# Issuing the second half's V gathers at twice the rate per step of their lane

## The chip, the cores and the metric

The kernel runs on one core of a Trainium2 chip. The metric is device time in microseconds (us), the median of several runs of one execution each; lower is better. Engines are named as in the profile: PE is TensorE (matmuls), PEld its weight loads, DVE is VectorE, ACT is ScalarE, POOL is GpSimd, SP is SyncE. DMAs are issued from the queues of SP, ACT and POOL; in this kernel SP issues the weights and most stores, POOL issues gathers and re-layouts.

## What is computed

One encoder block on 512 tokens (8 rows of 64) of width 1024, in float32. Cut to what matters here:

```python
x = x + 0.5 * swiglu(rmsnorm(x, norm_ffn1), w_ffn1_gu, w_ffn1_down)
h = rmsnorm(x, norm_mix)
xr, gr, q, k, v, ga, gb = split(h @ w_in, 7)
y_lru = (rglru_forward(conv(xr)) + rglru_backward(conv(xr))) * gelu(gr)
q, k = per-head rmsnorm of q and k
# for every query row, and for each of 4 blocks of 16 columns: scores against
# 8 rows x 32 columns of keys, a learned bias, a mask, softmax, then p @ v
y_att = neighbourhood_attention(q, k, v, rel_pos_bias)
x = x + (sigmoid(ga) * y_lru + sigmoid(gb) * y_att) @ w_out
x = x + 0.5 * swiglu(rmsnorm(x, norm_ffn2), w_ffn2_gu, w_ffn2_down)
```

There are 16 heads of 64 columns.

## The kernel before, in words

Every matmul is made of three float32r matmuls on a high and a low part (`mm3`, lines 171 to 174), so PE has most of the work. The middle of the kernel computes the projections of `w_in` one after the other and weaves two other pieces of work between their matmuls: the recurrence (`lru`) and the attention (`heads`). The parts of the middle that this change concerns run in this order:

1. Attention is done in two halves of 8 heads each (`hf` 0 and 1, the loop at the end of the attention code). For each half `qk_raw` computes q and k, `v_get` computes v, and `heads` is appended to a list of generators, the lane "att".
2. After both halves, `gates` computes 24 chunks of 24 matmuls of 128x512 (lines 172 to 174) for the gelu gate and the two merge gates, in phase "g". Between and in the middle of those chunks, `weave(RATE["g"])` advances the lanes. So the scores of the attention (line 950), its transposes (918, 920) and its products with V (1013) of the second half all stand between gate matmuls on PE.

A lane is a list of generators. Each call of `weave` adds the lane's rate to the lane's account, and for every whole unit in the account the generator is advanced by one step, that is to its next `yield`:

```python
    def weave(rate):
        for ln, n in rate.items():
            q = lanes[ln]
            due[ln] += n
            while due[ln] >= 1 and q:
                ...
                    next(q[0])
                    due[ln] -= 1
```

The lane "v" holds `v_more(hf)`. It gathers from DRAM the layouts of V that the attention's products need, since `v_get` leaves V there first (`vd`, line 860). It has seven steps. Steps 1 to 3 issue one gather each of 256 KB (`vs`, line 869). Then, for each of the two edge blocks of columns (n = 0, then n = 3), a buffer `te` is cleared by POOL (line 876) and two steps follow, each of which issues three gathers of 64 KB (`va` twice and `ve` once, line 880). All are issued from POOL's queue. For the first half all seven steps are taken at once (`until("v", lambda: False)`); for the second half they come by the rate of phase "g".

For one tile of heads `fi` (two heads, four such tiles in a half) the attention goes: `start` transposes q and k on PE; `scores` computes the scores on PE, DVE adds the bias `bm` (line 970), ACT takes the exponential (977), DVE scales (982); `ship` transposes 32x32 blocks on DVE (991, 992), stores the result to DRAM from SP's queue (`pd`, line 994) and reads it back from POOL's queue in four DMAs of 112 KB for each of the two blocks of columns (`PT`, line 998); `apply` multiplies it with V on PE (line 1013). One `apply` takes its columns in the order n = 0, 1, 2, 3: first `va` and `ve` of the left edge, then `vs`, then `va` and `ve` of the right edge. `bias` fetches the next tile's `bm` from POOL's queue (line 892). In the second half the `apply` of a tile stands two tiles of scores later (`ATT_LAG`).

What sets the order: PE, DVE, ACT, POOL and SP each run their instructions in one fixed order, which a scheduler makes from the order in which the code was written and from priorities. A POOL DMA that has to wait (for its source, for its buffer, or for room in the queue) holds up all that stand behind it on POOL. Buffers of the size of a tile come from one pool of 43 (`big_t`); there are five `PT` buffers and four `bm` buffers.

Of the kernel before, what the change touches and what calls it, by code (L numbers as in the profile page):

```python
# [83 lines left out]
    "xr": {"att": 0.0, "lru": 2.75},  # L84
    "t0": {"att": 0.0, "lru": 3.25},
    "t1": {"att": 0.75, "tail": 0.75, "lru": 2},
    "g": {"att": 0.7, "tail": 0.7, "lru": 1.5, "v": 0.25},
}


# [1123 lines left out]
```

## Time and profile before

| | us |
|---|---|
| median of 3 runs (lowest to highest) | 1114.73 (1114.38 to 1115.2) |
| the profiled execution, its own time | 1114.18 |
| its span, from first to last instruction | 1112.4 |
| DVE busy | 813.2 (73%) |
| ACT busy | 578.0 (52%) |
| POOL busy | 149.3 (13%) |

The mean granted TensorE clock over the span is 0.997. All instants below are microseconds from the start of the span. The gate matmuls of phase "g" run on PE from 550.7 to about 722. A row of the timeline gives the start, the duration, the engine, the line, the operation, its output and inputs, and, in brackets, how long the engine was idle before it and what ended the wait; "issue" means that the engine waited for nothing that the profile shows. A row of the windows view gives for one stretch the busy time of each engine, then the granted clock, the busy share of the DMA engines and the rate.

### The profile page before, as it was taken

What the parts mean: (1) busy time and instruction counts of PE and PEld (TensorE: products, weight loads), DVE (VectorE), ACT (ScalarE), POOL (GpSimd) and SP (SyncE); (2) the same over time, 40 slices, a digit from 0 to 9 for tenths busy, and PEclk for the clock granted to TensorE, in tenths of its full rate; (3) what the DMA queues carried; (4) which work ended last, traced back from release to release, by engine and by line L of the source; (5) the groups of instructions that cost most, each with busy time, mean ns of one, the idle gap of its engine ahead of it and who ended that gap; (6) DMA issues with size and microseconds to landing.
All of it is one profiled execution on the core that took longest, in us unless ns stands there. A gap on an engine that the chain in (4) does not pass through costs nothing.

```text
span 1112.4 us, 17673 instructions
## 1 busy us (share of the span) xinstructions
PE 1100.6 (99%) x6811; PEld 974.8 (88%) x6811; DVE 813.2 (73%) x1295; ACT 578.0 (52%) x871; POOL 149.3 (13%) x243
## 2 busy tenths in 40 slices
PE   9999999999999999999999979999999999999998
PEld 8899999988888778788888868889999999998887
DVE  7878777794745776999877956759877777785542
ACT  8554544563533679877454432346554454564330
POOL 0000000000000351230333542001000000000000
PEclk9999999999999999999999989999999999999999
DMA  8566666643423685573687655377766666553421
GB/s 267 153 169 152 150 156 167 159 147 95 133 82 107 168 255 152 167 210 106 211 260 184 195 176 160 104 239 160 199 146 158 157 166 147 157 170 95 133 76 38
DMA packets 64548, 175.93 MB, mean 158 GB/s; under 512 B 14544, under 2 KB 18384, under 8 KB 64464
## 3 DMA queue, kind: packets, MB, share of 16 engines
q1 hardware_dynamic: 43136, 127.75, 35.5%
q0 software_dynamic: 20752, 46.80, 21.0%
q8 instruction: 53, 0.87, 0.3%
q10 hardware_dynamic: 576, 0.26, 0.1%
q14 instruction: 31, 0.25, 0.1%
HBM read 150.53 MB, written 15.73 MB: 149 GB/s over the span
## 4 chain that ended last, share of the span: by engine, by line
PE 95%; issue 1%; DMA 1%; DVE 1%; POOL 1%; ACT 0%; ACTq 0%; POOLq 0%
PE acc L312 31%; PE acc L172 10%; PE acc L173 10%; PE acc L174 10%; PE aux L312 5%; PE acc L831 4%; PE acc L832 4%; PE acc L833 4%; PE aux L174 4%; PE aux L172 4%; PE aux L173 4%; PE aux L742 1%; PE aux L1013 1%; PE aux L950 1%; PE acc L464 1%
## 5 line engine op out<-in xcount | busy, mean ns | idle before, releaser
L145 ACT ACTIVATE wh<-wraw 128x1024 fp32r<-128x1024 f32 (+3 forms) x224 | 220.3, 988 | 304.2 <-issue 95.0
L148 DVE TENSOR_TENSOR wl<-wraw,wh 128x1024 fp32r<-128x1024 f32 (+3 forms) x236 | 267.0, 1136 | 100.1 <-ACT wh L145 98.8
L312 PE MATMUL acc<-s,wh 128*128 128x256 f32 x1280 | 232.2, 283 | 0.0
L312 PEld LDWEIGHTS acc<-s,wh 128*128 128x128 f32 x1280 | 199.7, 192 | 0.0
L312 PE MATMUL acc<-s,wl 128*128 128x256 f32 x640 | 181.1, 283 | 0.0
L312 PEld LDWEIGHTS acc<-s,wl 128*128 128x128 f32 x640 | 122.9, 192 | 0.0
L172 PE MATMUL acc<-xh,wh 128*128 128x512 f32 x272 | 107.5, 395 | 0.0
L174 PE MATMUL acc<-xh,wl 128*128 128x512 f32 x272 | 106.2, 391 | 0.0
L173 PE MATMUL acc<-xl,wh 128*128 128x512 f32 x272 | 106.1, 390 | 0.0
L312 PE MATMUL acc<-xl,wh 128*128 128x256 f32 x320 | 90.6, 283 | 0.0
L312 PE MATMUL acc<-xh,wl 128*128 128x256 f32 x320 | 90.6, 283 | 0.0
L312 PE MATMUL acc<-xh,wh 128*128 128x256 f32 x320 | 90.5, 283 | 0.0
L831 PE MATMUL acc<-wh,xh 128*128 128x512 f32 x192 | 75.7, 394 | 0.0
L832 PE MATMUL acc<-wh,xl 128*128 128x512 f32 x192 | 74.8, 389 | 0.0
L833 PE MATMUL acc<-wl,xh 128*128 128x512 f32 x192 | 74.8, 389 | 0.0
L148 DVE TENSOR_TENSOR hl<-h,hh 128x512 fp32r<-128x512 f32 x88 | 57.2, 687 | 21.7 <-PE aux L173 21.5
L172 PE MATMUL aux<-hh,wh 128*128 128x512 f32 (+1 forms) x181 | 69.9, 386 | 0.0
L173 PE MATMUL aux<-hl,wh 128*128 128x512 f32 (+1 forms) x181 | 69.9, 386 | 0.0
L174 PE MATMUL aux<-hh,wl 128*128 128x512 f32 (+1 forms) x181 | 69.9, 386 | 0.0
L174 PE MATMUL acc<-hh,wl 128*128 128x512 f32 (+1 forms) x176 | 67.9, 386 | 0.0
L173 PE MATMUL acc<-hl,wh 128*128 128x512 f32 (+1 forms) x176 | 67.9, 386 | 0.0
L172 PE MATMUL acc<-hh,wh 128*128 128x512 f32 (+1 forms) x176 | 67.9, 386 | 0.0
(221 smaller groups left out, 2297.6 us busy)
## 6 DMA issues: line engine op xcount, KB each, us to landing
wraw<-wqkv SPq DMA_DIRECT2D x24, 512.0 KB, 4.5
wraw<-wg SPq DMA_DIRECT2D x24, 512.0 KB, 7.4
wraw<-w1d SPq DMA_DIRECT2D x22, 512.0 KB, 3.7
wraw<-w2s SPq DMA_DIRECT2D x22, 512.0 KB
pair<-w2s SPq DMA_DIRECT2D x22, 512.0 KB, 4.4
wraw<-w2d SPq DMA_DIRECT2D x22, 512.0 KB, 3.6
wraw<-w1s SPq DMA_DIRECT2D x18, 512.0 KB, 3.5
pair<-w1s SPq DMA_DIRECT2D x18, 512.0 KB, 4.7
```

The source lines that it names most:

```text
L145: nc.scalar.activation(H, raw, AF.Copy)
L148: return nc.vector.tensor_tensor(L, raw, H.bitcast(F32), ALU.subtract)
L172: nc.tensor.matmul(ps, wh, xh, start=first, stop=False, skip_group_check=skip)
L173: nc.tensor.matmul(ps, wh, xl, start=False, stop=False, skip_group_check=skip)
L174: mark["mm"] = nc.tensor.matmul(ps, wl, xh, start=False, stop=last, skip_group_check=skip)
L312: mm = nc.tensor.matmul(o, w_[:, c], x_, start=first and m + k == 0 and w_ is H and x_ is xh_, stop=m + k == 4 and w_ is L, skip_group_che ...
L464: nc.tensor.matmul(pre[i], w[i][1][:, s], xh[k], start=k == 0, stop=False)
L742: prev, mm = mm, nc.tensor.matmul(ps[d][b], W[w][o, c], X[x][o], start=x == 1, stop=w + x == 0)
L831: nc.tensor.matmul(pss[j], xh[kk][:, tj], H[:, s], start=kk == 0, stop=False)
L832: nc.tensor.matmul(pss[j], xl[kk][:, tj], H[:, s], start=False, stop=False)
L833: mark["mm"] = nc.tensor.matmul(pss[j], xh[kk][:, tj], L[:, s], start=False, stop=kk == KT - 1)
L950: mm = hold(nc.tensor.matmul(ps[hp][:, cs], q_[o, n * P : (n + 1) * P], keys(k_[o]), start=k_ is kl, stop=q_ is ql))
```

## The change

One number in the table of rates: in phase "g" the lane of the V gathers gets 0.5 per call of `weave` instead of 0.25, so that a step is due at every second call, where it was due at every fourth. A gate chunk makes two calls, one in its middle and one behind it.

```diff
 RATE = {
     "xr": {"att": 0.0, "lru": 2.75},
     "t0": {"att": 0.0, "lru": 3.25},
     "t1": {"att": 0.75, "tail": 0.75, "lru": 2},
-    "g": {"att": 0.7, "tail": 0.7, "lru": 1.5, "v": 0.25},
+    "g": {"att": 0.7, "tail": 0.7, "lru": 1.5, "v": 0.5},
 }
```

On PE, ACT and SP the instructions stand in the same order as before, and on DVE two neighbours change places (a block transpose of line 991 and a split of line 148). On POOL the order changes from the third tile of heads of the first half to the second tile of the second. The rows below are POOL's, in the order of the program; `x4` stands for four DMAs in a row, and the numbers are those of buffers, which differ between the two programs. The first place is around the last `PT` of the first half (`PT_6013` before, `PT_6017` now). Before:

```order
L998 DMA PT_5901<-pd_5899 128x1x224 x4
L892 DMA bm_6325<-rpb 128x640
L869 DMA vs_6018<-vd_82 128x1x512
L892 DMA bm_6327<-rpb 128x640
L869 DMA vs_6111<-vd_82 128x1x512
L998 DMA PT_6013<-pd_6011 128x1x224 x4
L892 DMA bm_6540<-rpb 128x640
L892 DMA bm_6542<-rpb 128x640
L876 MEMSET ve_6330 128x512
L880 DMA va_6329<-vd_82 64x4x64 x2
```

And at the same place now:

```order
L892 DMA bm_6343<-rpb 128x640
L876 MEMSET ve_6023 128x512
L880 DMA va_6022<-vd_82 64x4x64 x2
L880 DMA ve_6023<-vd_82 64x4x64
L880 DMA va_6022<-vd_82 64x4x64 x2
L880 DMA ve_6023<-vd_82 64x4x64
L892 DMA bm_6345<-rpb 128x640
L876 MEMSET ve_6123 128x512
L880 DMA va_6122<-vd_82 64x4x64 x2
L880 DMA ve_6123<-vd_82 64x4x64
L880 DMA va_6122<-vd_82 64x4x64 x2
L998 DMA PT_6017<-pd_6015 128x1x224 x4
```

Eleven of the twelve edge gathers and both clears, which stood behind the first half's last `PT`, now stand ahead of it. The two `vs` that stood just ahead of it have moved further up, ahead of `PT_5684` and `PT_5903`.

The second place is around the `PT` of the second half's first two tiles of heads (`PT_6292` and `PT_6302`, then `PT_6507`, before; `PT_6310` and `PT_6320`, then `PT_6516`, now). Before:

```order
L998 DMA PT_6292<-pd_6290 128x1x224 x4
L998 DMA PT_6302<-pd_6300 128x1x224 x4
L892 DMA bm_6770<-rpb 128x640
L892 DMA bm_6772<-rpb 128x640
L876 MEMSET ve_6609 128x512
L880 DMA va_6608<-vd_82 64x4x64 x2
L880 DMA ve_6609<-vd_82 64x4x64
L880 DMA va_6608<-vd_82 64x4x64 x2
L880 DMA ve_6609<-vd_82 64x4x64
L998 DMA PT_6507<-pd_6505 128x1x224 x4
L998 DMA PT_6517<-pd_6515 128x1x224 x4
```

And now:

```order
L880 DMA ve_6123<-vd_82 64x4x64
L892 DMA bm_6549<-rpb 128x640
L892 DMA bm_6551<-rpb 128x640
L998 DMA PT_6310<-pd_6308 128x1x224 x4
L998 DMA PT_6320<-pd_6318 128x1x224 x4
L892 DMA bm_6770<-rpb 128x640
L892 DMA bm_6772<-rpb 128x640
L998 DMA PT_6516<-pd_6514 128x1x224 x4
L998 DMA PT_6526<-pd_6524 128x1x224 x4
```

The right edge's clear and its six gathers have left the place between `PT_6302` and `PT_6507`; the two `bm` that stood ahead of the left edge's gathers (`bm_6540`, `bm_6542`) now stand just ahead of the second half's first `PT`.

## The prediction, written before the changed kernel ran

> **What bounds the kernel now.** I read the page first, then who PE waits for, then PE's own rows around that wait.
>
> ```profile
> PE 1100.6 (99%) x6811; PEld 974.8 (88%) x6811; DVE 813.2 (73%) x1295; ACT 578.0 (52%) x871; POOL 149.3 (13%) x243
> PE 95%; issue 1%; DMA 1%; DVE 1%; POOL 1%; ACT 0%; ACTq 0%; POOLq 0%
> PE aux L1013 <- DMA va<-vd: 6.9, 2, 4.7
> PE aux L138 <- DVE pol L667: 1.1, 1, 1.1
> ```
>
> PE is busy 99% of the span, and the chain that ended last is 95% PE. So the time changes only where PE's waits or its clock change. The view of waits (total, times, longest) has two for PE in the whole kernel: 1.1 us at the start, and 6.9 us in two pieces in the attention's product (line 1013), for a `va` gather. This is the only place where a change of DMA order alone can gain anything. PE's timeline there:
>
> ```profile
> 639.38 0.44 PE L1013 MATMUL aux<-PT,va 128*64 128x128 f32 x4
> 639.65 0.39 PE L1013 MATMUL aux<-PT,ve 128*64 128x128 f32 x4
> 639.87 1.04 PE L1013 MATMUL aux<-PT,vs 128*64 128x128 f32 x16
> 645.64 0.66 PE L1013 MATMUL aux<-PT,va 128*64 128x128 f32 x2 [4.72 <-DMA va<-vd]
> 648.49 0.44 PE L1013 MATMUL aux<-PT,va 128*64 128x128 f32 x1 [2.20 <-DMA va<-vd]
> ...
> 651.99 0.40 PE L173 MATMUL acc<-xl,wh 128*128 128x512 f32 x1
> ```
>
> It is the second half's first `apply`. Left edge and middle go through at once; at the right edge PE stands 4.72 and then 2.20 us until the gathers of that edge land. POOL's timeline says why they are late:
>
> ```profile
> 606.21 0.66 POOL L998 DMA_DIRECT2D PT<-pd  x1 [3.37 <-issue]
> ...
> 613.65 1.61 POOL L880 DMA_DIRECT2D va<-vd  x2
> ...
> 624.48 2.02 POOL L998 DMA_DIRECT2D PT<-pd  x3 [5.09 <-DMA pd<-pt]
> ...
> 633.09 1.44 POOL L998 DMA_DIRECT2D PT<-pd  x2 [2.38 <-issue]
> 634.52 1.47 POOL L892 DMA_DIRECT2D bm<-rpb  x2
> ...
> 636.44 0.81 POOL L880 DMA_DIRECT2D va<-vd  x1
> ...
> 646.57 0.77 POOL L880 DMA_DIRECT2D ve<-vd  x1
> 647.80 0.69 POOL L998 DMA_DIRECT2D PT<-pd  x1 [0.46 <-issue]
> ```
>
> The left edge's six were issued from 613.65, in time. The right edge's six stand behind eight `PT` and two `bm` and were issued from 636.44 to 646.57, when PE needed them at 640.7.
>
> **The wait's price.** The wait costs more than 6.92, since PE also runs slower behind it:
>
> ```profile
> 640.00:644.00 4.00, 0.92 (x18) 0.67 (x14) 3.62 (x20) 2.10 (x10) 1.05 (x2) 1.00 0.82 282
> 644.00:652.00 8.00, 4.09 (x18) 2.98 (x19) 0.31 (x2) 1.87 (x6) 4.34 (x6) 0.57 0.30 71
> 652.00:656.00 4.00, 4.00 (x19) 3.32 (x18) 2.87 (x5) 1.87 (x3) 1.96 (x3) 1.00 0.53 152
> ```
>
> The granted clock (third number from the end) is 0.57 from 644 to 652 and 1.00 on both sides. So I price the passage as a whole, against the same work where nothing is late:
>
> ```profile
> 623.49 0.66 PE L918 MATMUL aux<-ident,qk 128*128 128x128 f32 x4
> ...
> 624.67 0.44 PE L1013 MATMUL aux<-PT,va 128*64 128x128 f32 x4
> ...
> 664.43 0.44 PE L1013 MATMUL aux<-PT,va 128*64 128x128 f32 x4
> ...
> 666.33 0.50 PE L172 MATMUL acc<-xh,wh 128*128 128x512 f32 x1
> 666.67 0.39 PE L173 MATMUL acc<-xl,wh 128*128 128x512 f32 x1
> ```
>
> An `apply` takes 666.33 - 664.43 = 1.90, the eight transposes of `start` 624.67 - 623.49 = 1.18, and from the first gate matmul to the second it is 0.34: 3.42 together. The late passage has the same work from 639.38 to 651.99, that is 12.61. The loss is **9.19 us**: 6.92 of waiting and 2.27 of slow clock.
>
> **What the change does, part by part.** No instruction is added or removed; PE, ACT and SP keep their order. On DVE two neighbours change places; the view of waits has no wait of PE's for DVE in this phase, so I take 0. On POOL the right edge's gathers leave the place behind `PT_6302` and go ahead of the first half's last `PT`. Three things follow.
>
> First, the right edge. How fast twelve such gathers go through the queue is seen in the first half, where they are issued in one row:
>
> ```profile
> 485.20 1.57 POOL L880 DMA_DIRECT2D va<-vd  x2
> ...
> 501.55 0.77 POOL L880 DMA_DIRECT2D ve<-vd  x1
> DMA to landing us min/median/max: 2.5/4.3/8.0
> ```
>
> From 485.20 to 502.32 are 17.1 us for twelve, 15.7 for eleven. They can begin when the `PT` ahead of them are out (before: the last was issued at 591.21) and a `bm` and a clear have gone, so at about 594 to 597. The last of them is then issued at 610 to 613, or some 620 with the `PT` in between, and has landed by 628 even with the longest landing of `va`, 8.0. PE needs it at 640.7. The margin is 12 us, so the wait of 6.92 goes, and the slow clock with it: **-9.19**.
>
> Second, what now stands behind the gathers: the first half's last `PT` (four DMAs). The rows are two of POOL's, the landing of all `PT` (shortest, median, longest), a stretch seen on POOL alone (busy time, clock, DMA share, GB/s), and PE's use.
>
> ```profile
> 591.21 0.66 POOL L998 DMA_DIRECT2D PT<-pd  x1 [0.21 <-issue]
> ...
> 596.42 0.70 POOL L998 DMA_DIRECT2D PT<-pd  x1
> DMA to landing us min/median/max: 3.2/4.7/9.4
> 604.00:608.00 4.00, 0.66 (x1) 1.00 0.22 48
> 625.13 1.07 PE L1013 MATMUL aux<-PT,vs 128*64 128x128 f32 x16
> ```
>
> Before, they took from 596.42 to 606.87 and PE used them at about 625.4, in the middle of the first half's last `apply`. Now they start at 610 to 613. Four took 10.4 us there, in a crowded stretch; the eight from 624.48 to 634.53 took 10.0, so 5 for four. Issue ends between 615 and 623, and with the median landing of 4.7 they are there between 620 and 628. Between these ends (0 and +2.6) I take 0: the DMA engines were busy only 0.22 of the time from 604 to 608, so the gathers that move there find room, and the faster rate is the nearer one.
>
> Third, the second half's `PT`. All eight from 624.48 on were needed by about 640.4, in the middle of the `apply` that begins at 639.38. The rows are the landing of the last two of them, that of a `bm` at a quiet time (count, size, median landing), and SP's two pairs of stores that these `PT` and the next tile's wait for:
>
> ```profile
> DMA to landing us min/median/max: 5.9/6.0/6.1
> bm<-rpb POOLq DMA_DIRECT2D x2, 320.0 KB, 3.2
> 618.21 1.38 SPq L994 DMA_DIRECT2D pd<-pt  x2
> 634.27 1.38 SPq L994 DMA_DIRECT2D pd<-pt  x2
> ```
>
> The last two were issued from 633.09 to 634.53, so the last was there at 639.7, just before its use. Now two `bm` stand right ahead of these eight and compete with the store that they wait for. The bounds are 0 and 6.4, two `bm` one after the other. POOL stood 5.09 us for that store before 624.48, which leaves the `bm` a place, so I am near the lower end: **+0.7**. Then the next tile's `PT` (`PT_6516`, `PT_6526`). Before, they began at 647.80, held up by the gathers, and were needed by 665.4, half an `apply` behind 664.43. With PE 9.2 earlier they are needed by 656.2. They can begin once their store has landed. The store of 618.21 released POOL at 624.48, 6.3 later, so that of 634.27 does at 640.6. Eight took 15.2 from the first issue to the last landing (624.48 to 639.7). That gives 655.8, a tie; bounds 0 and 3 (the crowded rate), I take **+0.5**.
>
> Does the gain reach the end? DVE is what is late next, if anything:
>
> ```profile
> 651.69 0.17 DVE L979 RECIPROCAL rs<-rs 128x2 f32<-128x2 f32 x1 [7.70 <-ACT p L977]
> 600.00:640.00 40.00, 39.92 (x285) 32.91 (x286) 35.11 (x99) 19.27 (x49) 16.42 (x24) 1.00 0.64 184
> ```
>
> DVE itself stood 7.70 us, because ACT stood behind PE's late `apply`; it is busy 35.11 of 40 us ahead of the place. So it keeps pace, and behind 652 PE waits for nobody.
>
> **The sum.** 1114.18 (the profiled execution, 1112.4 of span and 1.8 around it) - 9.19 + 0 + 0.7 + 0.5 = 1106.2. The median of the runs shown is 0.55 above that execution; I forecast a little above the sum, **1106.5**.
>
> [...] The gathers move from a stretch in which DVE is idle into one in which it is 88% busy. By the rows, a `va` issued at 636.44, with DVE busy, took 0.81, and the `ve` at 646.57, with DVE idle, 0.77: eleven times 0.04 is 0.4 us on POOL, none of it on PE's path. [...]
>
> **The rivals.** (a) The wait moves instead of going: the second half's `PT` come late at 639.4 or 655.3, by 3 to 7 us instead of 1.2. For it: the margins of 0.5 and 0.3 above. Against it: POOL loses six gathers ahead of the second group. Time 1114.18 - 9.19 + 3 to 7 = 1108 to 1112. (b) Slower: the first half's last `PT`, now behind eleven gathers, lands so late that PE stands at 625.4 for longer than it gains. It decides from 625.4 + 9.2 = 634.6 on, plus the slow clock if PE stands for long, as at 640. From 595 that would be 39.6 us for eleven gathers, four `PT` and a landing, where the rows give 15.7 + 10.4 + 4.7 = 30.8 at the slow end. At 9.4 of landing and a third more for each gather it is 40.7, PE stands for 10.3, the slow clock adds 2.3: 1114.18 - 9.19 + 12.6 = 1117.6. (c) Nothing changes, because the new waits at the three places add up to the gain, or the right edge waits for something that the trace of before does not show: 1113 to 1115. The change does do what it says, as POOL's order shows, so that is no rival.
>
> [...]
>
> **How the numbers follow.** Forecast (new waits of 0 to 3 us): 0.75, 1105.0 to 1108. Rival (a): 0.12. Rival (b): 0.06. Rival (c): 0.07. The range from 1104.6 to 1110.5 has the forecast and more than half of (a), 0.82. A measurement of this kernel can tell about 0.2%, 2.2 us, from no change. Faster by more: the forecast and nearly all of (a), 0.86; within: 0.07; slower: 0.07.
>
> **What would show it.** Right: PE's wait for `va` is gone from the view of waits, the granted clock is 1.00 from 640 to 656, the gathers of line 880 are issued between 594 and 625, and the next `apply` begins at about 655.3 instead of 664.43. Wrong: a wait of PE's at line 1013 for `PT<-pd`, at 625, 640 or 655, of more than 2 us; DVE waiting for `bm`; or any new wait of PE's behind 660. The longest of these is also what separates (a), (b) and (c).

## The result, and the profile after

Over 20 runs each, the changed kernel took 1108.09 us in the median (1105.87 to 1114.74) and the kernel before 1115.32 (1113.79 to 1118.47). The medians lie 7.2 us apart; the ratio over all runs is 0.9942, 95% interval 0.993 to 0.9953, which is some 6.5 us. The forecast was 1106.5 with a range from 1104.6 to 1110.5. Two things strike the eye: the median lies 1.6 us above the forecast, and the runs now spread over 9 us where those of before spread over 5. The mean granted clock of the 20 runs goes with that spread: twelve of them had 1.000 and took 1105.87 to 1109.75 us, eight had 0.995 to 0.998 and took 1109.15 to 1114.74.

The run that was profiled is the slowest of the 20, 1114.74 us with a span of 1113.0 and a clock of 0.995. It isn't typical, but it shows magnified what holds the others back. First the page's line of busy times, and the view of PE's waits (total, times, longest).

```profile
PE 1102.2 (99%) x6811; PEld 976.0 (88%) x6811; DVE 813.4 (73%) x1295; ACT 578.1 (52%) x871; POOL 148.9 (13%) x243
```

```profile
PE aux L1013 <- DMA PT<-pd: 5.8, 2, 3.7
PE aux L138 <- DVE pol L667: 1.1, 1, 1.1
PE aux L1013 <- PE aux L920: 0.3, 1, 0.3
```

The wait for `va`, 6.9 us before, is gone. In its place stand two waits for `PT`, of 5.8 us together. Where they are is seen in PE's timeline (start, duration, and in brackets the idle time ahead with what ended it).

```profile
639.18 0.44 PE L1013 MATMUL aux<-PT,va 128*64 128x128 f32 x4
...
642.41 0.66 PE L1013 MATMUL aux<-PT,vs 128*64 128x128 f32 x8 [2.13 <-DMA PT<-pd]
...
658.69 0.44 PE L1013 MATMUL aux<-PT,va 128*64 128x128 f32 x4
...
674.42 0.44 PE L1013 MATMUL aux<-PT,va 128*64 128x128 f32 x4
...
684.70 0.44 PE L1013 MATMUL aux<-PT,va 128*64 128x128 f32 x4
...
689.48 1.12 PE L1013 MATMUL aux<-PT,vs 128*64 128x128 f32 x8 [3.69 <-DMA PT<-pd]
```

These are the second half's four applies. The first stands 2.13 us for the second `PT` of its pair, the last 3.69. The second begins at 658.69 instead of 664.43, not at 655.3 as forecast. Beside the wait, the windows show why (busy time of PE, PEld, DVE, ACT and POOL with counts; then the granted clock, the DMA share and GB/s): the clock falls behind both waits.

```profile
640.00:644.00 4.00, 1.87 (x25) 1.49 (x22) 3.46 (x18) 2.34 (x10) 1.73 (x3) 0.94 0.94 314
644.00:652.00 8.00, 8.00 (x34) 6.71 (x33) 4.94 (x9) 3.33 (x8) 2.22 (x4) 0.82 0.46 132
...
688.00:692.00 4.00, 2.52 (x18) 2.10 (x19) 0.00 (x0) 0.50 (x2) 0.00 (x0) 0.50 0.09 35
692.00:700.00 8.00, 8.00 (x31) 6.49 (x30) 3.21 (x4) 2.19 (x4) 0.00 (x0) 0.83 0.11 24
```

POOL's timeline shows the gathers where the prediction put them, and behind them the `PT` in groups of three and two.

```profile
598.41 1.59 POOL L880 DMA_DIRECT2D va<-vd  x2
...
621.46 0.81 POOL L880 DMA_DIRECT2D ve<-vd  x1 [2.64 <-issue]
622.27 1.16 POOL L892 DMA_DIRECT2D bm<-rpb  x2
625.02 2.04 POOL L998 DMA_DIRECT2D PT<-pd  x3 [1.59 <-PE aux L1013]
630.14 1.98 POOL L998 DMA_DIRECT2D PT<-pd  x3 [3.08 <-issue]
634.80 1.82 POOL L998 DMA_DIRECT2D PT<-pd  x2 [2.68 <-issue]
```

Three go out in 2 us, then POOL stands some 3 us "for nothing that the profile shows", and three more go out. That is the trail which the experiments follow.

**A measure for all runs.** Two stretches of PE hold the same work in every kernel here. A runs from the first row of the second half's first apply to that of its second, B from the first row of the last apply to the end of the span. In the profiled execution of `r8_after_ring3072` below they are 15.5 and 422.0 us with no wait in them. Before, A is 664.43 - 639.38 = 25.05 and B 1112.4 - 690.44 = 421.96, so its whole loss is 9.5 us in A. After, A is 658.69 - 639.18 = 19.5 and B 1113.0 - 684.70 = 428.3, a loss of 4.0 and 6.3: 5.8 of waiting and 4.5 of slow clock. In this one execution the old loss of 9.5 was exchanged for a new one of 10.3.

### The profile page after: what moved, and what is told of

The parts are those of the page before. It is cut to its first block, busy times and chain, and to the rows that moved or that the text cites. A ratio compares the mean times of both kernels' runs of the same rounds, so it can differ in the third digit from the quotient of the medians.

```text
span 1113.0 us, 17676 instructions
## 1 busy us (share of the span) xinstructions
PE 1102.2 (99%) x6811; PEld 976.0 (88%) x6811; DVE 813.4 (73%) x1295; ACT 578.1 (52%) x871; POOL 148.9 (13%) x243
## 3 DMA queue, kind: packets, MB, share of 16 engines
HBM read 150.53 MB, written 15.73 MB: 149 GB/s over the span
## 4 chain that ended last, share of the span: by engine, by line
PE 95%; issue 2%; DMA 1%; POOL 1%; DVE 0%; ACTq 0%; POOLq 0%; ACT 0%
PE acc L312 31%; PE acc L172 10%; PE acc L173 10%; PE acc L174 10%; PE aux L312 5%; PE acc L831 4%; PE acc L832 4%; PE acc L833 4%; PE aux L172 4%; PE aux L174 4%; PE aux L173 4%; PE aux L742 1%; DMA PT<-pd 1%; POOL PT L998 1%; PE aux L1013 1%
```

## The experiments

**My theory.** The rest of the gain is lost in waits for `PT`, because POOL's queue has room for only about three of these DMAs at a time: a next one goes out when one of the three has landed. **Rivals**: the two `bm` that now stand right ahead of the first `PT`; the DMA engines or the store of `pd`, which would set the pace with any queue; the clock by itself; the gathers' place still.

**1. The changed kernel again, for a run near the median (`r1_after_again`).** No edit.

> The changed kernel once more. My theory: what is missing of the 9.19 us is lost in waits of PE for PT at line 1013, at the second half's first and last apply (2.13 and 3.69 us in the profiled run of 1114.74), and in the slow clock behind them; a run nearer the median of 1108.1 then shows the same waits at the same places, but shorter, or without the slow stretch behind them: 1106 to 1110, waits of 2 to 5 us in all. Rival, clock alone: the waits are the same 5.8 us as in the profiled run and only the granted clock differs.

It took 1108.24 us (ratio to before 0.9935, 0.9923 to 0.9947), and the profiled execution 1106.93. PE's waits, its rows and two windows:

```profile
PE aux L1013 <- DMA PT<-pd: 1.9, 2, 1.3
```

```profile
639.10 0.44 PE L1013 MATMUL aux<-PT,va 128*64 128x128 f32 x4
...
641.45 0.66 PE L1013 MATMUL aux<-PT,vs 128*64 128x128 f32 x8 [1.25 <-DMA PT<-pd]
...
656.08 0.44 PE L1013 MATMUL aux<-PT,va 128*64 128x128 f32 x4
...
682.30 0.44 PE L1013 MATMUL aux<-PT,va 128*64 128x128 f32 x4
...
684.02 0.66 PE L1013 MATMUL aux<-PT,vs 128*64 128x128 f32 x8 [0.62 <-DMA PT<-pd]
```

```profile
644.00:652.00 8.00, 8.00 (x37) 6.62 (x36) 6.13 (x11) 2.38 (x5) 2.54 (x4) 1.00 0.64 185
...
688.00:692.00 4.00, 4.00 (x20) 3.30 (x18) 1.92 (x2) 0.95 (x1) 0.00 (x0) 1.00 0.19 27
```

The same two places, no slow stretch, and waits a little shorter than the 2 to 5 us that I had expected: A 17.0, B 422.8, a loss of 1.5 and 0.8. The clock by itself is thereby out: it is 1.00 where the waits are short, and what is missing is still missing at the waits. In the profiled run of the result, with a mean clock of 0.995, slow stretches came on top.

**2. Half of the second half's `PT` on SP (`r2_half_pt_on_sp`), and the same in the kernel before (`r3_before_half_pt_on_sp`).**

```diff
-                nc.gpsimd.dma_start(PT[:, j].rearrange("p q i -> p (q i)"), ...
+                (nc.sync if hf == 1 and j % 2 else nc.gpsimd).dma_start(PT[:, j].rearrange("p q i -> p (q i)"), ...
```

> The changed kernel, with two of the four PT read-backs of each second-half tile issued by SP instead of POOL; PE, DVE and ACT keep their order. My theory (about three of these DMAs are under way on POOL's queue at a time, so eight take 15 us however early PE is): PE's waits for PT fall below 1 us, the last PT lands some 3 us or more before 689.4, and the time is 1105.0, 1104 to 1106. Rival, the store of pd or the crowded DMA engines set the landing: the last PT still lands at about 689, the waits stay, 1108. Rival, clock alone: 1108 with no waits. Price if SP's weight loads are held up behind its wait for the store: a new wait of PE or DVE for wraw, above 1108.

It took 1114.56 us (0.9994, 0.9985 to 1.0003): the gain was gone. The wait at the first apply went, as expected (A is 654.66 - 639.16 = 15.5), but at the last apply PE stood longer than ever, and B is 1111.8 - 680.94 = 430.9:

```profile
639.16 0.44 PE L1013 MATMUL aux<-PT,va 128*64 128x128 f32 x4
...
654.66 0.44 PE L1013 MATMUL aux<-PT,va 128*64 128x128 f32 x4
...
680.94 0.44 PE L1013 MATMUL aux<-PT,va 128*64 128x128 f32 x4
...
688.26 1.12 PE L1013 MATMUL aux<-PT,vs 128*64 128x128 f32 x8 [6.24 <-DMA PT<-pd]
```

SP's timeline shows the price, and not where I had looked for it (in the weights):

```profile
654.37 0.38 SPq L994 DMA_DIRECT2D pd<-pt  x1
663.07 1.11 SPq L998 DMA_DIRECT2D PT<-pd  x2
...
664.75 0.43 SPq L994 DMA_DIRECT2D pd<-pt  x1
...
672.08 1.11 SPq L998 DMA_DIRECT2D PT<-pd  x2
673.24 0.49 SPq L994 DMA_DIRECT2D pd<-pt  x1
...
680.25 1.11 SPq L998 DMA_DIRECT2D PT<-pd  x2
```

SP stands for the landing of each store before it can issue that store's `PT` (34.3 us in six waits, the longest 8.2, by the view of SP's waits), and the next store is queued behind it. So the stores go out one after the other, 8.5 to 10.4 us apart, the last at 673.24 (664.80 in `r1_after_again`). As a test of the queue's room this run is spoiled: it gave with one hand and took with the other.

> The kernel before, with the same two of four PT read-backs on SP. My theory: the right edge's gathers now stand behind four PT instead of eight on POOL and are issued 4 to 5 us earlier, so PE's wait for va shrinks from 6.9 to 2 or 3 us and no wait for PT follows: 1109, 1107 to 1112. Rival, only the gathers' place ahead of the PT matters: the wait for va stays near 6.9, 1114 to 1115.

It took 1115.11 us (0.9997, 0.9989 to 1.0006), so my expectation was wrong. The right edge's first two gathers went out earlier (632.94 instead of 636.44), yet the last only at 642.16, since POOL stood 1.29, 2.67 and 1.29 us between them for nothing that the profile shows, and PE went on with it at 648.06: PE stood 4.7 us for `ve` and 1.8 for `va`. Four `PT` less on POOL were not enough.

**3. The lane's rate at 1.0 (`r4_v_rate_1`).**

```diff
-    "g": {"att": 0.7, "tail": 0.7, "lru": 1.5, "v": 0.5},
+    "g": {"att": 0.7, "tail": 0.7, "lru": 1.5, "v": 1.0},
```

> The rate of the lane doubled once more, to 1.0: all gathers stand ahead of the first half's last two PT. My theory: the va wait is gone already and the second half's PT and bm stand as before, so nothing is left to gain: 1108, 1106.5 to 1110. Rival (b) of the prediction, the first half's last PT come late behind the gathers: a wait of PE for PT at about 625, 1110 or more. Rival, the gathers' place is still what costs: 1105.

1109.93 us (0.9952, 0.9938 to 0.9966), with 4.1 us of waits for `PT` in two pieces, 1.72 at 642 and 2.36 at 686, and none at 625. So the gathers' place gives nothing more, and the waits for `PT` are there with it too.

**4. The six bias loads on SP (`r7_after_bm_on_sp`).**

```diff
-            ld = nc.gpsimd.dma_start(bms[g, hp], a["rpb"][g * 2 + hp])
+            ld = (nc.sync if g >= 5 else nc.gpsimd).dma_start(bms[g, hp], a["rpb"][g * 2 + hp])
```

> The changed kernel with the six bias loads of the second half's later tiles (bm, 320 KB each) issued by SP; PE, DVE and ACT keep their order. Rival theory that I take seriously: the two bm that now stand right ahead of the first PT are what makes PE wait at 641 (1.25 and 2.13 us); then the first PT are issued at 623 instead of 625.2, the wait at the first apply goes, and the time is 1105.5 to 1107. My theory (room on POOL's queue in general): the wait at the first apply shrinks too, the one at the last apply stays at 0 to 3 us; 1106 to 1108. Price, if SP stands for a bm buffer and the stores of pd come later: above 1108.

1107.21 us (0.9932, 0.9918 to 0.9946), not to be told apart from the 0.9935 of the changed kernel. PE's waits:

```profile
PE aux L1013 <- DMA PT<-pd: 2.6, 2, 1.9
```

0.68 us of them are at the first apply and 1.87 at the last. The first wait was 1.25 and 2.13 us in the two traces with the `bm` on POOL, so they may account for part of it, but without them both waits are still there: as the whole cause, they are out.

**5. More room on POOL's queue (`r5_after_ring4096`, `r6_before_ring4096`, `r8_after_ring3072`, `r9_before_ring3072`).** The kernel sets `dynamic_dma_scratch_size` itself, the space in the table below. The expectations take it for the space of the descriptors of POOL's DMAs; the traces show no descriptors, they show how many DMAs are under way with each value. In these four only that number changes, and every engine keeps its order; with 4096, `rq`, a small tile of the attention, has one buffer instead of two.

```diff
-    nc = bacc.Bacc("TRN2", target_bir_lowering=False, num_devices=1, dynamic_dma_scratch_size=2048)
+    nc = bacc.Bacc("TRN2", target_bir_lowering=False, num_devices=1, dynamic_dma_scratch_size=4096)
```

> The changed kernel with the space for the descriptors of POOL's DMAs doubled (4096 for 2048; rq gives up its second buffer to make room); every engine keeps its order. My theory (PT wait for one another on POOL because only about three such DMAs have room at a time): the gaps between the PT issues fall from some 1.9 to below 1 us, PE's waits for PT (1.9 us in the second run of the changed kernel, 5.8 in the first) go, and the runs lie close together: 1105.0, 1104 to 1106. Rival, the DMA engines or the store of pd set the pace: more are under way, each takes longer, the last PT still lands at 684 or later, 1107 to 1108.5. Rival, the clock: no change.

> The kernel before with the same doubled space. My theory: the right edge's gathers no longer wait for room behind the eight PT; they are issued by 636 instead of 646.6, PE's wait for va shrinks from 6.9 us to 0 to 3, and the time is 1105 to 1109, without the change. Rival, the gathers' place behind the PT is the cause in itself: wait near 6.9, 1114 to 1115.

> The changed kernel with half as much room again for the descriptors of POOL's DMAs (3072 for 2048), and rq with both its buffers. My theory: with 2048 at most 3 of the PT and gathers were under way, with 4096 at most 7; here 5. Eight PT then take 5 issues, a landing of 5 us and 3 more, some 11 us instead of 15, the last PT lands at about 680, ahead of its use at 681, and the time is 1104.3 to 1105.5. If the second buffer of rq or another effect of the doubled space had made the gain, it stays near 1108.

> The kernel before with 3072. My theory: the right edge's gathers are issued by about 641 (646.6 with room for three, 636.7 with room for seven) and land by 645, so PE still waits for va or ve at 641, by 2 to 4 us, and the slow clock may follow: 1106.5 to 1111. Here the change should still pay, by 2 to 5 us against the changed kernel with the same room. Rival, any room beyond three is enough: 1104.8 as with 4096.

| space | before (rate 0.25) | changed (rate 0.5) | PT and gathers under way, at most |
|---|---|---|---|
| 2048 | 1115.3 | 1108.2 | 3 |
| 3072 | 1112.47 (1108.07 to 1113.15) | 1104.24 (1104.22 to 1104.64) | 5 |
| 4096 | 1104.79 (1104.67 to 1107.15) | 1104.26 (1104.16 to 1104.46) | 7 |

The last column is counted from the issue and the landing of each of these DMAs between 590 and 695 us in the traces; it is the same for both kernels of a row. The `bm` and `vs`, which go through the same queue, are not in it: with them up to six were under way at 2048. The ratios to the kernel before are 0.9902 (0.9887 to 0.9917) for `r8_after_ring3072`, 0.9906 (0.9893 to 0.992) for `r5_after_ring4096`, 0.9917 (0.9903 to 0.993) for `r6_before_ring4096` and 0.9969 (0.9956 to 0.9982) for `r9_before_ring3072`.

With 4096 the changed kernel issues seven `PT` in one row, where it was three (POOL's timeline of `r5_after_ring4096`):

```profile
623.59 4.65 POOL L998 DMA_DIRECT2D PT<-pd  x7 [10.68 <-PE acc L950]
629.42 0.68 POOL L998 DMA_DIRECT2D PT<-pd  x1 [1.18 <-DMA PT<-pd]
```

The traces with 2048 also show what ended POOL's idle time. In `r1_after_again` there are 26 pieces of it without a visible cause ahead of a `PT` or a gather in this stretch, and each ends 0.13 to 0.34 us after a `PT` or a gather has landed. What POOL stood for nothing visible, ahead of its `PT` between 590 and 695 us, was 32.2 us in 20 pieces in `r1_after_again`:

```profile
POOL PT L998 <- issue: 32.2, 20, 4.5
```

and in `r5_after_ring4096`:

```profile
POOL PT L998 <- issue: 1.4, 2, 1.2
```

The landing did not get longer in return by much (all 64 `PT`, size and median), 4.7 us in `r1_after_again`:

```profile
PT<-pd POOLq DMA_DIRECT2D x64, 112.0 KB, 4.7
```

and 5.4 in `r5_after_ring4096`:

```profile
PT<-pd POOLq DMA_DIRECT2D x64, 112.0 KB, 5.4
```

So it was the room and not the DMA engines or the stores: with more under way, about the same landing, and the last `PT` there at 676.4 instead of 684.0 by the traces (issued at 670.15 instead of 679.87). The DMA engines are near full for a few microseconds with either space (their busy share is 0.93 from 640 to 644 in `r1_after_again` and 0.97 from 652 to 656 in `r8_after_ring3072`), and in the second no wait is left all the same. 3072 does the same with `rq` untouched, so `rq` has no part in it. PE's rows of `r8_after_ring3072`:

```profile
639.40 0.44 PE L1013 MATMUL aux<-PT,va 128*64 128x128 f32 x4
...
654.91 0.44 PE L1013 MATMUL aux<-PT,va 128*64 128x128 f32 x4
...
670.63 0.44 PE L1013 MATMUL aux<-PT,va 128*64 128x128 f32 x4
...
680.91 0.44 PE L1013 MATMUL aux<-PT,va 128*64 128x128 f32 x4
```

No wait for `PT` is left in it. A is 15.5, B is 1102.9 - 680.91 = 422.0. The first apply begins at 639.40, at 639.38 before, and B is that of before: ahead of 639 and behind the last apply the room changes nothing, all of the gain lies between.

In the kernel before, room for five is not enough; the waits are the 2 to 4 us that I expected, but the time lies above my 1111, since I had let the slow clock follow without pricing it in full. One run of the seven, at a clock of 1.000, took 1108.07; the other six, at 0.996 or 0.997, took 1110.7 to 1113.15. The right edge's gathers, behind eight `PT` and two `bm`, still come late, and PE's rows show three short waits instead of two long ones, with the slow clock behind them (PE's timeline and a window of `r9_before_ring3072`):

```profile
642.25 0.40 PE L1013 MATMUL aux<-PT,va 128*64 128x128 f32 x2 [0.98 <-DMA va<-vd]
643.98 0.29 PE L1013 MATMUL aux<-PT,va 128*64 128x128 f32 x1 [1.33 <-DMA va<-vd]
...
646.02 0.69 PE L1013 MATMUL aux<-PT,ve 128*64 128x128 f32 x2 [1.51 <-DMA ve<-vd]
```

```profile
644.00:652.00 8.00, 6.49 (x23) 5.16 (x24) 3.68 (x10) 2.67 (x7) 4.84 (x8) 0.57 0.63 159
```

With room for seven they are out in one row, and the wait for `va` is gone without the change; 1104.79 us is just below the 1105 to 1109 that I had expected (POOL's timeline of `r6_before_ring4096`):

```profile
632.04 1.64 POOL L880 DMA_DIRECT2D va<-vd  x2
633.67 0.77 POOL L880 DMA_DIRECT2D ve<-vd  x1
634.43 1.53 POOL L880 DMA_DIRECT2D va<-vd  x2
635.95 0.81 POOL L880 DMA_DIRECT2D ve<-vd  x1
```

By the medians the change is thus worth 7.1 us with room for three, 8.2 with five, where I had expected 2 to 5, and 0.5 with seven. With seven the two sets of runs do not overlap (1104.46 at most against 1104.67 at least), but 0.35 of the 0.5 us between the two traces lies ahead of the second half's first apply (639.06 and 639.41), and PE waits for no DMA in either; so it is not shown that the gathers' place makes that difference. The old wait and the new ones have one cause, the room on POOL's queue; the change moved the gathers out of its way, and the `PT` stayed in it.

The changed kernel with 3072 is faster than both kernels of this case: 1104.24 us, and its four runs lie within 0.4 us, where the changed kernel's 20 spread over 9 and its five of `r1_after_again`, on another chip, over 2.4.

## Why the prediction was right, and where not

- **The wait for `va`, -9.19: right.** It is gone from every trace with the rate at 0.5 or 1.0. The whole passage, without any wait, is 15.5 us (`r8_after_ring3072`) against 25.05 before: 9.5, where the sum had 9.19 from the pieces. 1114.18 less that is 1104.6, and 1104.24 is what was measured once the `PT` were out of the way.
- **The gathers' issue, between 594 and 625: right.** 598.41 to 621.46 in the profiled run.
- **The first half's last `PT`, 0: right.** No trace has a wait for `PT` at 625. Rival (b) didn't come, and neither did it with the rate at 1.0. The 24 gathers of the two traces of the changed kernel took 0.77 to 0.88 us to issue, but for one of 1.19, with DVE busy for 19.11 of the 24 us from 598 to 622 in the profiled run and 23.09 of the 28 from 596 to 624 in `r1_after_again`; before, the twelve took 0.77 to 0.83, the last three of them with DVE idle (0.31 us busy from 644 to 652).
- **The first tile's `PT`, +0.7: mis-sized.** The place was right, and the bounds of 0 to 6.4 held it; the loss in A was 1.5 us in `r1_after_again` and 4.0 in the profiled run, slow clock included. I priced the two `bm`, which `r7_after_bm_on_sp` shows to be a part at most: 0.68 us of wait is left without them. The room of three, which the rows of before showed already as groups of three, I used only to reckon how long eight `PT` take.
- **The next tile's `PT`, +0.5: 0.** The second apply had no wait of note in any run: A ends on time once its own `PT` are there.
- **"Behind 652 PE waits for nobody": this is the step that failed.** I looked at DVE there, and not at the rest of the `PT`. The rows of before had it (PE's timeline of `before`):

```profile
680.16 0.44 PE L1013 MATMUL aux<-PT,va 128*64 128x128 f32 x4
...
690.44 0.44 PE L1013 MATMUL aux<-PT,va 128*64 128x128 f32 x4
```

The second half's applies follow one another by 15.73 us (664.43 to 680.16) but the last by 10.28 (680.16 to 690.44), and eight `PT` took 15.2. Before, the last `PT` landed at 689.59 by the trace, 0.9 us ahead of the apply that began at 690.44 and uses it in its second half: PE could not come 9.2 us earlier there unless the `PT` did too. After, they landed at 689.44 in the profiled run and at 684.0 in `r1_after_again`, and PE stood 3.69 and 0.62 us.

- **The signs of being wrong: two of them came.** In the profiled run PE waited 2.13 us for a `PT` at 640, where more than 2 was the mark, and both traces of the changed kernel have a new wait of PE's behind 660. The clock, which was to be 1.00 from 640 to 656, was so in `r1_after_again` and fell to 0.82 in the profiled run.
- **Rival (a), "the wait moves", 1108 to 1112, had 0.12: too little.** By its mechanism it is what happened, in part, in both traces of the changed kernel, though by 1.25 and 2.13 us at the first place, less than its 3, and with the second wait at a place that it did not name. Of the 20 runs 11 lie at 1108 or above, and eight of these had a clock below 1.000. Its argument against, that POOL loses six gathers ahead of the second group, was true and beside the point. The margins that it calls 0.5 and 0.3 are 0.7 (639.7 to 640.4) and 0.4 (655.8 to 656.2) by the prediction's own instants; nothing else hangs on them.

The forecast of 1106.5 was thus near for a mixed reason: a term of the right size, and two new waits of which one was foreseen too small and the other not at all. That the time stayed within the range was in part luck, since no bound of the sum stood for the wait at the last apply.

**Left open**: what decides in a given run whether the last `PT` land at 684 or at 689. In the profiled run PE was 2.6 us later at the second apply than in `r1_after_again`, but the last `PT` 5.5 us later; the other 2.9 I cannot trace to one place. Over all 64 `PT` the landing took 5.3 us in the median there and 4.7 in `r1_after_again`. That the spread shrinks with more room was seen (2.4 us in five runs with 2048, 0.4 in four with 3072), and that it goes with the granted clock too; why some executions get the lower clock and others don't was not. A place for half of the `PT` on SP behind the next store, which would mend what spoiled `r2_half_pt_on_sp`, was not tried.

## What to carry to other kernels

When a wait for a DMA goes, the consumer is earlier at every later place too (PE at the last apply at 680.91 in `r8_after_ring3072`, at 690.44 before): check each later stream that it consumes, with its last landing in the trace and the shortest distance between two uses, not only the next one and not only engines. When a queue issues in groups of the same size with gaps that nothing explains, first find out what limits the number under way; here a `dynamic_dma_scratch_size` of 4096 was worth more than the better order (1104.79 us with the old order, 1108.2 with the new one at 2048), and it made the order matter less (0.5 us instead of 7.1). And before moving a read-back to an in-order queue, see what stands behind it there: SP's wait for one store held up the next, which went out 8.5 to 10.4 us apart.

## What the runs showed of the hardware

- On POOL's queue the `PT` (112 KB) and the gathers (64 KB) were at most 3, 5 and 7 under way with 2048, 3072 and 4096 of space, in eleven executions. The three are not a bound on DMAs of every kind, since up to six were under way at 2048 with the `bm` and `vs`; how much of the space each kind takes was not measured.
- The slow clock did not follow the length of a single wait: 0.82 from 644 to 652 behind 2.13 us in the profiled run, 1.00 behind 1.72 and behind 2.36 us in `r4_v_rate_1`, and 0.57 behind three waits of 0.98, 1.33 and 1.51 us within 5 us in `r9_before_ring3072`. What sets it was not shown: outcomes differ for like waits.
